# Second retention pair's queries and keys as one seven-product group, with the input sums formed in the first pair

## The chip, the cores and the metric

The kernel runs on one core of a Trainium2 chip. The metric is the device time of one execution in microseconds; the kernel before took 1776.57 us (median of 3 runs, 1776.14 to 1777.71). The engines of the core are named as in the profile: PE (matmul) and PEld (its weight loads), DVE (vector), ACT (activation), POOL (GpSimd) and SP, from whose queue the weights are loaded.

## What is computed

A trunk of two layers on 512 tokens of width 1024, in float32. A layer makes one combined projection `x @ w_in`, whose columns are split among two branches. The part that matters here is the retention branch with 4 heads of query and key width 128 and value width 256, which comes first in a layer:

```python
def _rotary(x, pos):
    half = x.shape[-1] // 2
    ...
    x1, x2 = x[..., :half], x[..., half:]
    return jnp.concatenate([x1 * cos - x2 * sin, x1 * sin + x2 * cos], axis=-1)
...
rq = _rotary(r_q.astype(f32).reshape(B, S, RET_HEADS, RET_QK_DIM), pos)
rk = _rotary(r_k.astype(f32).reshape(B, S, RET_HEADS, RET_QK_DIM), pos) * (RET_QK_DIM ** -0.5)
rv = r_v.astype(f32).reshape(B, S, RET_HEADS, RET_V_DIM)
o_ret = _head_norm(_retention(rq, rk, rv), ret_norm_g[l]) * jax.nn.silu(r_g.astype(f32))
```

The second branch (mLSTM) has queries and keys from a causal convolution, values, and an input and a forget gate per head (`m_i`, `m_f`, from the same projection). Both branches are gated, projected, added, normalised, and followed by a SwiGLU block and a second normalisation.

## The kernel before, in words

**Three matmuls for one.** Each float32 operand is split into a high part (a copy in the matmul's reduced format: `xh`, `whi`) and a low part (the difference: `xl`, `wlo`). A product is the sum of three matmuls: high by high, high by low, low by high (lines 266 to 268, 324, 357 to 359). ACT makes the high parts (line 201), DVE the low parts (`lo_of`, line 133).

**Weight units.** All weights lie in DRAM as units of 128 x 1024 (512 KB), in the order of use (`layer_plan`). A feature unit (`feat`, line 272) gives 128 output features for all 512 tokens: 24 matmuls of 512 columns into one PSUM bank, with a slot (below) after every sixth. A token unit (`tok_units`, line 361) is used by four blocks of 128 tokens: 6 matmuls and one slot for each block. `take` and `used` (lines 231 and 237) keep a ring of 5 raw and 5 prepared weight tiles running, some 4 units ahead.

**Seven products instead of eight.** `quad` (line 304) computes four feature units as a 2 x 2 block product with seven products in place of eight (in the manner of Strassen and Winograd). It loads four blocks of weights in place of four units (`QUADS`, `QUAD_BLOCKS`), forms three weight sums on DVE (lines 187, 189, 191) and one on POOL (line 223), and prepares seven operands in place of four. A product has 24 matmuls of 256 columns and two slots. On the other side it needs four sums of the input, `xs` (`input_sums`, line 580). A callback `ev` combines the banks after each product. Inside a quad the instructions of ACT, DVE and POOL keep the order of the program (`manual_schedule(engines=ordered)`). Before the change the quad is used for the mLSTM's queries and keys, for the two merge gates and for the SwiGLU units.

**The input sums.** `input_sums` is a generator with four groups (m = 0 to 3). Each group first adds high and low parts on POOL (2 instructions of line 586, tile `xs`), yields, then forms four sums on DVE (4 instructions of line 592, tile `sf`), casts them on ACT (line 593, `xs0h` in layer 0, `xs1h` in layer 1), takes the low half on DVE (line 133, `xs0l`, `xs1l`) and yields again.

**Order of the work.** PE and SP run in program order. On ACT, DVE and POOL a planner at compile time orders the instructions by its own estimate of when each is ready, and prefers the ones that stand earlier in the program. Smaller work is put between the matmuls by slots: `slot()` (line 246) takes the next step of a queue `side` and, at every `SLOW`-th slot, one step of a queue `slow`. `drain()` empties `side`. Only the input sums use `slow`.

**A layer's retention.** Heads go in pairs, p = 0 and 1. For a pair: four feature units (q, k of either head), each rotated out of its PSUM bank (`rot_evac`, lines 615 to 617 on DVE, 618 on POOL); for p = 0 the gate unit (`feat_if`) with a long chain of small operations on tile `rows` (`if_evac`, lines 632 to 662); four value token units (value stage), whose four PSUM banks are evacuated by ACT (`rvh`) and DVE (`rvl`); four gate token units (gate stage), into the same four banks of the pool `psm`, evacuated by ACT (line 732). Meanwhile `side` holds the first head's scores (`scores`, line 456), for p = 0 twelve empty steps and the transposes of the gate rows (`if_cols`, line 668), and in the gate stage the weighted sums of the first head, the scores of the second head and its weighted sums (`weighted`, line 495). The head norm of a pair (`head_norms`, with 16 transposes on line 547) runs in the slots of whatever comes next. The input sums are queued at the start of p = 1 and used first by the mLSTM's first quad.

Of the kernel before, what the change touches and what calls it, by code (L numbers as in the profile page):

```python
# [13 lines left out]
ALU = mybir.AluOpType  # L14

P = 128
S = 512
# [36 lines left out]
def layer_plan():  # L54
# [34 lines left out]
    for j in range(2, FT, 2):  # L89
        for c in (0, DFF):  # L90
# [5 lines left out]


NUNIT = len(layer_plan())
QUADS = [layer_plan().index(("F", w, c + j * P)) for w, c, js in (("in", O_MQK, (0, 2)), ("in", O_GA, (0, 4)),
                                                                  ("in", O_GB, (0, 4)), ("gu", 0, range(2, FT, 2))) for j in js]  # L100
UNIT_IF = layer_plan().index(("F", "if", 0))

# [2 lines left out]
def decoder_trunk(ctx: ExitStack, tc: tile.TileContext, wall, xT_in, x_in, pvec, lnp, rtab, out):  # L105
    nc = tc.nc
# [17 lines left out]
    def scratch(shape, name):  # L124
        return reg.tile(shape, F32, tag="sc", name=name, bufs=4)
# [12 lines left out]
    for l in range(L):  # L138
        i = 0
# [100 lines left out]


    side, slow = deque(), deque()
    SLOW = 5
    turn = {"n": 0}

    def slot():
# [333 lines left out]
    def input_sums(xh, xl, sh, sl):  # L580

        t1, t2 = slice(0, S // 2), slice(S // 2, S)
        for m in range(4):
            t = scratch([P, 2, S], "xs")
            for i in range(2):
                nc.gpsimd.tensor_tensor(out=t[:, i], in0=xh[:, m + 4 * i].bitcast(F32), in1=xl[:, m + 4 * i].bitcast(F32), op=ALU.add)
            yield
            f = scratch([P, 4, S // 2], "sf")
            a11, a12, a21, a22 = t[:, 0, t1], t[:, 1, t1], t[:, 0, t2], t[:, 1, t2]
            for i, a, b, op in ((0, a21, a22, ALU.subtract), (1, f[:, 0], a11, ALU.subtract),  # L590
                                (2, a11, a21, ALU.subtract), (3, f[:, 1], a12, ALU.add)):
                nc.vector.tensor_tensor(out=f[:, i], in0=a, in1=b, op=op)
            nc.scalar.copy(sh[:, :, m], f)
            lo_of(sl[:, :, m], f, sh[:, :, m])
            yield

    def rest(n):
        for _ in range(n):
            yield

    for l in range(L):
# [7 lines left out]
        xs = sum_views(oth, f"xs{l}")  # L609
        od = [dr.tile([P, KT, S], F32, tag=f"od{i}", name="od") for i in range(2)]  # L610

        def rot_evac(dst):
            def ev(pm):
                t = scratch([P, S], "rt")
                nc.vector.tensor_tensor(out=dst, in0=pm, in1=tab[:, 0], op=ALU.mult)
                nc.vector.tensor_tensor(out=t[0:64], in0=pm[64:128], in1=tab[0:64, 1], op=ALU.mult)
                nc.vector.tensor_tensor(out=t[64:128], in0=pm[0:64], in1=tab[64:128, 1], op=ALU.mult)
                nc.gpsimd.tensor_tensor(out=dst, in0=dst, in1=t, op=ALU.add)
            return ev

        def split_evac(vh, vl, hh, b, src):
            nc.scalar.copy(vh, src)
# [48 lines left out]
            yield  # L671

        for p in range(2):
            if p == 1:
                slow.append(input_sums(xh, xl, *xs))
            qk = reg.tile([P, 4, S], F32, tag="qk", name="rqk")
            rots = [rot_evac(qk[:, i]) for i in range(4)]
            if p == 0 and l > 0:
                feat_split(xh, xl, rots, between)
            elif p == 0:  # L680
                first_units(rots)
            else:
                for ev in rots:
                    feat(xh, xl, ev)
            if p == 0:
                feat_if(xh, xl, if_evac)
            boxes = [[None], [None]]

            def ret_weights(h):
# [62 lines left out]
                                               op0=ALU.mult, op1=ALU.add)  # L752
            nc.scalar.activation(x, t, AF.Silu)

        def conv_ev(qk):
            t = {}
            part = lambda i, h: qk[:, 2 * i : 2 * i + 2, h * HC : (h + 1) * HC]
            two = lambda bank: bank.rearrange("p (j t) -> p j t", j=2)

            def ev(name, banks):  # L760
                if name == "p1":
                    t["u"] = scratch([P, 2, 2, HC], "mu")
                    nc.scalar.copy(t["u"][:, 0], two(banks["a"]))
                elif name == "p5":
                    nc.scalar.copy(t["u"][:, 1], two(banks["c"]))
                elif name == "p7":
                    nc.vector.tensor_tensor(out=part(1, 1), in0=t["u"][:, 1], in1=two(banks["d"]), op=ALU.subtract)
                elif name == "p6":
                    u, v = t["u"][:, 0], t["u"][:, 1]
                    nc.vector.tensor_tensor(out=u, in0=two(banks["b"]), in1=u, op=ALU.add)  # L770
                    nc.gpsimd.tensor_tensor(out=v, in0=v, in1=u, op=ALU.subtract)
                    nc.gpsimd.tensor_tensor(out=part(1, 1), in0=part(1, 1), in1=u, op=ALU.subtract)
                elif name == "p2":
                    nc.scalar.copy(part(0, 0), two(banks["a"]))
                    nc.vector.tensor_tensor(out=part(1, 0), in0=two(banks["e"]), in1=t["u"][:, 1], op=ALU.add)
                elif name == "p4":
                    nc.vector.tensor_tensor(out=part(0, 1), in0=two(banks["d"]), in1=t["u"][:, 0], op=ALU.add)
            return ev

        for p in range(2):  # L780
            qk = reg.tile([P, 4, S], F32, tag="qk", name="mqk")
            with tc.manual_schedule(engines=ordered):
                quad(xh, xl, *xs, conv_ev(qk))
            for i in range(4):
                conv(qk[:, i], (i % 2) * 4 + 2 * p + i // 2)
            side.append(rest(7))
# [444 lines left out]
```

## Time and profile before

| | |
|---|---|
| median of 3 runs | 1776.57 us (1776.14 to 1777.71) |
| the profiled execution | 1777.92 us, span 1776.2 us |
| PE busy | 1759.9 us of the span |
| DVE busy | 1312.9 us |
| ACT busy | 793.6 us |
| POOL busy | 433.3 us |
| mean granted clock of PE | 0.998 |

The profile is of one execution. Its span runs from the first to the last instruction, and the execution's own time lies a little above it. In timelines a row has the start, the duration (both in us), the engine, the line of the kernel, the operation and its tiles, and, in brackets, how long the engine stood idle in front of it and what released it. Matmuls overlap, so the distance between the starts of two rows tells their rate, not the duration. In the views of groups the durations are in ns.

### The profile page before, as it was taken

Reading aid. Unit: us, or ns where it says so; the run is one execution under the profiler, and the core shown is the slowest. Engines: PE = TensorE matmul, PEld = TensorE weight load, DVE = VectorE, ACT = ScalarE, POOL = GpSimd, SP = SyncE. Lnnn points to the kernel's source line nnn. Section 1 sums busy time; section 2 is a strip of 40 time slices with the busy share of each in tenths; the row PEclk is TensorE's granted clock in tenths of the full one; section 3 lists DMA queues with packets and bytes.
Section 4 is the critical chain, followed back from the end, with each engine's and each line's share of the span. In section 5 each row is a group of like instructions: output and inputs, shape, how many; then the busy total and the mean of one; then the engine's idle time right before and its main releaser. Section 6 shows DMA issues by size and latency. Waiting matters only on the chain.

```text
span 1776.2 us, 27128 instructions
## 1 busy us (share of the span) xinstructions
PE 1759.9 (99%) x10904; PEld 1586.3 (89%) x10904; DVE 1312.9 (74%) x1726; ACT 793.6 (45%) x1148; POOL 433.3 (24%) x321
## 2 busy tenths in 40 slices
PE   9999999999999999999999999999999999999997
PEld 7888898998889999988898898989988899999886
DVE  6676878795559999963476968787845699998534
ACT  4445555663226444451244455556533254445310
POOL 2141110231001555520121311113300115555200
PEclk9999999999999999999999999999999999999999
DMA  7232422346333323363242323313553223333521
GB/s 250 86 105 72 143 72 96 106 137 239 96 111 110 105 96 108 107 213 95 83 166 89 110 88 106 119 60 108 200 180 119 95 95 108 111 116 114 186 69 48
DMA packets 74878, 209.48 MB, mean 118 GB/s; under 512 B 6616, under 2 KB 8536, under 8 KB 73728
## 3 DMA queue, kind: packets, MB, share of 16 engines
q1 hardware_dynamic: 64912, 168.32, 29.6%
q0 software_dynamic: 9840, 39.43, 6.3%
q8 instruction: 86, 1.41, 0.3%
q14 instruction: 40, 0.33, 0.1%
HBM read 190.93 MB, written 16.79 MB: 117 GB/s over the span
## 4 chain that ended last, share of the span: by engine, by line
PE 97%; DVE 1%; ACT 0%; issue 0%; DMA 0%; SPq 0%; DVEq 0%
PE pm L324 31%; PE pm L357 9%; PE pm L359 9%; PE pm L358 9%; PE pm L266 6%; PE pm L268 6%; PE pm L267 6%; PE pa L324 5%; PE pa L358 3%; PE pa L357 3%; PE pa L359 3%; PE pa L491 1%; PE pa L492 1%; PE pa L493 1%; PE pa L547 1%; PE pa L465 1%
## 5 line engine op out<-in xcount | busy, mean ns | idle before, releaser
L133 DVE TENSOR_TENSOR wlo<-wraw,whi 128x1024 fp32r<-128x1024 f32 (+2 forms) x416 | 599.6, 1453 | 203.1 <-ACT whi L201 200.5
L201 ACT CAST whi<-wraw 128x1024 fp32r<-128x1024 f32 x403 | 421.1, 1049 | 476.2 <-PE pm L267 116.0
L447 POOL TENSOR_TENSOR rs<-ve,nhalf 128x4 f32<-128x4 f32 (+1 forms) x32 | 33.0, 1033 | 480.2 <-DVE ve L446 480.2
L223 POOL TENSOR_TENSOR wraw<-wraw 128x1024 f32<-128x1024 f32 x32 | 77.0, 2405 | 150.9 <-issue 58.1
L357 PE MATMUL pm<-whi,x0h 128*128 128x512 f32 x256 | 102.5, 400 | 1.8 <-DVE rvl L133 1.7
L357 PE MATMUL pm<-whi,x20h 128*128 128x512 f32 x256 | 102.5, 400 | 0.6 <-DVE rvl L133 0.6
L359 PE MATMUL pm<-wlo,x0h 128*128 128x512 f32 x256 | 100.3, 392 | 0.0
L359 PE MATMUL pm<-wlo,x20h 128*128 128x512 f32 x256 | 100.3, 392 | 0.0
L358 PE MATMUL pm<-whi,x20l 128*128 128x512 f32 x256 | 100.1, 391 | 0.0
L358 PE MATMUL pm<-whi,x0l 128*128 128x512 f32 x256 | 100.1, 391 | 0.0
L1082 POOL TENSOR_TENSOR qa<-qa 128x512 f32<-128x512 f32 x20 | 42.8, 2142 | 142.3 <-DVE qa L1081 90.4
L324 PE MATMUL pm<-x10h,whi 128*128 128x256 f32 x240 | 67.9, 283 | 0.0
L324 PE MATMUL pm<-x10l,whi 128*128 128x256 f32 x240 | 67.9, 283 | 0.0
L324 PE MATMUL pm<-s0h,whi 128*128 128x256 f32 x240 | 67.9, 283 | 0.0
L324 PE MATMUL pm<-s0l,whi 128*128 128x256 f32 x240 | 67.9, 283 | 0.0
L324 PE MATMUL pm<-s0h,wlo 128*128 128x256 f32 x240 | 67.9, 283 | 0.0
L324 PE MATMUL pm<-x11h,whi 128*128 128x256 f32 x240 | 67.9, 283 | 0.0
L324 PE MATMUL pm<-x11l,whi 128*128 128x256 f32 x240 | 67.9, 283 | 0.0
L324 PE MATMUL pm<-x11h,wlo 128*128 128x256 f32 x240 | 67.9, 283 | 0.0
L324 PE MATMUL pm<-s1h,whi 128*128 128x256 f32 x240 | 67.9, 283 | 0.0
L324 PE MATMUL pm<-s1l,whi 128*128 128x256 f32 x240 | 67.9, 283 | 0.0
L324 PE MATMUL pm<-s1h,wlo 128*128 128x256 f32 x240 | 67.9, 283 | 0.0
(519 smaller groups left out, 5672.5 us busy)
## 6 DMA issues: line engine op xcount, KB each, us to landing
wraw<-wall SPq DMA_DIRECT2D x307, 512.0 KB, 3.8
od<-ot POOLq DMA_DIRECT2D x16, 512.0 KB, 3.6
of<-od POOLq DMA_DIRECT2D x16, 512.0 KB, 4.8
gb<-lnp POOLq DMA_DIRECT2D x4, 1024.0 KB, 6.3
x1d<-xr POOLq DMA_DIRECT2D x8, 512.0 KB, 3.0
xr<-x1d POOLq DMA_DIRECT2D x8, 512.0 KB, 4.6
negm<-md POOLq DMA_DIRECT2D x2, 1026.0 KB, 6.3
xr<-xtok POOLq DMA_DIRECT2D x4, 512.0 KB, 7.4
```

Source lines behind the costliest of these rows:

```text
L133: nc.vector.tensor_tensor(out=out_lo, in0=full, in1=hi.bitcast(F32), op=ALU.subtract)
L201: nc.scalar.copy(hi, sum_t[i])
L223: nc.gpsimd.tensor_tensor(out=raw_t[u + 2], in0=raw_t[u], in1=raw_t[u + 3], op=ALU.add)
L266: nc.tensor.matmul(pm[:, c0:c1], lhsT=hi[:, k], rhs=xh[:, k, c0:c1], start=(k == 0), stop=False)
L267: nc.tensor.matmul(pm[:, c0:c1], lhsT=hi[:, k], rhs=xl[:, k, c0:c1], start=False, stop=False)
L268: nc.tensor.matmul(pm[:, c0:c1], lhsT=lo[:, k], rhs=xh[:, k, c0:c1], start=False, stop=(k == KT - 1))
L324: nc.tensor.matmul(pm, lhsT=x[:, j, k], rhs=y[:, k], start=go and n == 0, stop=j == 1 and k == 3 and n == 2, skip_group_check=not first)
L357: nc.tensor.matmul(pm, lhsT=sh(k)[:, a], rhs=hi[:, j], start=first, stop=False)
L358: nc.tensor.matmul(pm, lhsT=sl(k)[:, a], rhs=hi[:, j], start=False, stop=False)
L359: nc.tensor.matmul(pm, lhsT=sh(k)[:, a], rhs=lo[:, j], start=False, stop=last)
L447: nc.gpsimd.tensor_tensor(out=rs[:, :n], in0=ve[:, :n], in1=nhalf[:, :n], op=ALU.pow)
L1082: nc.gpsimd.tensor_tensor(out=v, in0=v, in1=u, op=ALU.subtract)
```

## The change

The four feature units of the second retention pair (p = 1) become one `quad`. The callback that was `conv_ev` is now called `blocks_ev`, stands earlier in the layer and is used for both; it leaves the plain queries and keys in `qk`. After the quad the four are rotated in place, from SBUF, by the new `rotate`, which `rot_evac` of the first pair uses too, with the products of the swapped halves first. Seven empty steps (`rest(7)`) are put into `side` before the scores, as the mLSTM has them. The quad's units are added to `QUADS`, so that its weights are loaded in blocks. Since the quad needs the input sums, these are queued in p = 0, right after `feat_if`, and with a step at every third slot in place of every fifth; an assertion says that they are queued completely before the quad.

```diff
-QUADS = [layer_plan().index(("F", w, c + j * P)) for w, c, js in (("in", O_MQK, (0, 2)), ("in", O_GA, (0, 4)),
+QUADS = [layer_plan().index(("F", w, c + j * P)) for w, c, js in (("in", O_RQ, (2,)), ("in", O_MQK, (0, 2)), ("in", O_GA, (0, 4)),
...
-    SLOW = 5
+    SLOW = 3
...
+        def blocks_ev(qk):
...
+        def rotate(dst, x):
+            t = scratch([P, S], "rt")
+            nc.vector.tensor_tensor(out=t[0:64], in0=x[64:128], in1=tab[0:64, 1], op=ALU.mult)
+            nc.vector.tensor_tensor(out=t[64:128], in0=x[0:64], in1=tab[64:128, 1], op=ALU.mult)
+            nc.vector.tensor_tensor(out=dst, in0=x, in1=tab[:, 0], op=ALU.mult)
+            nc.gpsimd.tensor_tensor(out=dst, in0=dst, in1=t, op=ALU.add)
+
         def rot_evac(dst):
-            def ev(pm):
-                t = scratch([P, S], "rt")
-                nc.vector.tensor_tensor(out=dst, in0=pm, in1=tab[:, 0], op=ALU.mult)
...
+            return lambda pm: rotate(dst, pm)
...
         for p in range(2):
-            if p == 1:
-                slow.append(input_sums(xh, xl, *xs))
...
             else:
-                for ev in rots:
-                    feat(xh, xl, ev)
+                assert not slow
+                with tc.manual_schedule(engines=ordered):
+                    quad(xh, xl, *xs, blocks_ev(qk))
+                for i in range(4):
+                    rotate(qk[:, i], qk[:, i])
+                side.append(rest(7))
             if p == 0:
                 feat_if(xh, xl, if_evac)
+                slow.append(input_sums(xh, xl, *xs))
...
-        def conv_ev(qk):
...
-                quad(xh, xl, *xs, conv_ev(qk))
+                quad(xh, xl, *xs, blocks_ev(qk))
```

The callback, unchanged but for its name and place:

```python
def blocks_ev(qk):
    t = {}
    part = lambda i, h: qk[:, 2 * i : 2 * i + 2, h * HC : (h + 1) * HC]
    two = lambda bank: bank.rearrange("p (j t) -> p j t", j=2)
    def ev(name, banks):
        if name == "p1":
            t["u"] = scratch([P, 2, 2, HC], "mu")
            nc.scalar.copy(t["u"][:, 0], two(banks["a"]))
        elif name == "p5":
            nc.scalar.copy(t["u"][:, 1], two(banks["c"]))
        elif name == "p7":
            nc.vector.tensor_tensor(out=part(1, 1), in0=t["u"][:, 1], in1=two(banks["d"]), op=ALU.subtract)
        elif name == "p6":
            u, v = t["u"][:, 0], t["u"][:, 1]
            nc.vector.tensor_tensor(out=u, in0=two(banks["b"]), in1=u, op=ALU.add)
            nc.gpsimd.tensor_tensor(out=v, in0=v, in1=u, op=ALU.subtract)
            nc.gpsimd.tensor_tensor(out=part(1, 1), in0=part(1, 1), in1=u, op=ALU.subtract)
        elif name == "p2":
            nc.scalar.copy(part(0, 0), two(banks["a"]))
            nc.vector.tensor_tensor(out=part(1, 0), in0=two(banks["e"]), in1=t["u"][:, 1], op=ALU.add)
        elif name == "p4":
            nc.vector.tensor_tensor(out=part(0, 1), in0=two(banks["d"]), in1=t["u"][:, 0], op=ALU.add)
    return ev
```

More of the change, by code (lines that the diff above doesn't have):

```diff
@@ L610, in decoder_trunk, with ev @@
         od = [dr.tile([P, KT, S], F32, tag=f"od{i}", name="od") for i in range(2)]
-        def rot_evac(dst):
-            def ev(pm):
-                t = scratch([P, S], "rt")
[L615 to L619, printed above, removed]
+        def blocks_ev(qk):
+            t = {}
+            part = lambda i, h: qk[:, 2 * i : 2 * i + 2, h * HC : (h + 1) * HC]
+            two = lambda bank: bank.rearrange("p (j t) -> p j t", j=2)
+            def ev(name, banks):
+                if name == "p1":
+                    t["u"] = scratch([P, 2, 2, HC], "mu")
+                    nc.scalar.copy(t["u"][:, 0], two(banks["a"]))
+                elif name == "p5":
+                    nc.scalar.copy(t["u"][:, 1], two(banks["c"]))
+                elif name == "p7":
+                    nc.vector.tensor_tensor(out=part(1, 1), in0=t["u"][:, 1], in1=two(banks["d"]), op=ALU.subtract)
+                elif name == "p6":
+                    u, v = t["u"][:, 0], t["u"][:, 1]
+                    nc.vector.tensor_tensor(out=u, in0=two(banks["b"]), in1=u, op=ALU.add)
+                    nc.gpsimd.tensor_tensor(out=v, in0=v, in1=u, op=ALU.subtract)
+                    nc.gpsimd.tensor_tensor(out=part(1, 1), in0=part(1, 1), in1=u, op=ALU.subtract)
+                elif name == "p2":
+                    nc.scalar.copy(part(0, 0), two(banks["a"]))
+                    nc.vector.tensor_tensor(out=part(1, 0), in0=two(banks["e"]), in1=t["u"][:, 1], op=ALU.add)
+                elif name == "p4":
+                    nc.vector.tensor_tensor(out=part(0, 1), in0=two(banks["d"]), in1=t["u"][:, 0], op=ALU.add)
+            return ev
@@ L753, in conv @@
             nc.scalar.activation(x, t, AF.Silu)
-        def conv_ev(qk):
[L756 to L778, printed above, removed]
         for p in range(2):
```

## The prediction

> **What bounds the kernel now.** I read the page's first part first, then the matrix engine's waits, then timelines of the places that the diff touches, then a table of busy time by stretches.
>
> ```profile
> span 1776.2 us, 27128 instructions
> PE 1759.9 (99%) x10904; PEld 1586.3 (89%) x10904; DVE 1312.9 (74%) x1726; ACT 793.6 (45%) x1148; POOL 433.3 (24%) x321
> ```
>
> PE is busy for all but 16.3 us of the span. So the kernel can get faster by little except by less matrix work, and it gets slower by every microsecond in which another engine lets PE wait. Where PE waits for another engine today, the waits view says in its first row:
>
> ```profile
> PE pm L357 <- DVE rvl L133: 2.3, 2, 1.7
> ```
>
> Two waits, one per layer, both of the same kind: the first matmul of the gate units of the first retention pair waits for DVE, which still has to write the low half of the values (rvl) before the PSUM bank is free. The PE timeline at that place, first layer, then second layer:
>
> ```profile
> 59.49 0.39 PE L359 MATMUL pm<-wlo,x0h 128*128 128x512 f32 x1
> 60.09 0.44 PE L668 MATMUL pa<-ident,rows 36*128 36x36 f32 x4 [0.21 <-DVE rows L659]
> 62.27 0.50 PE L357 MATMUL pm<-whi,x0h 128*128 128x512 f32 x1 [1.74 <-DVE rvl L133]
> ```
> ```profile
> 941.60 0.50 PE L357 MATMUL pm<-whi,x20h 128*128 128x512 f32 x1 [0.58 <-DVE rvl L133]
> ```
>
> And DVE in front of it (first layer):
>
> ```profile
> 49.74 0.68 DVE L644 TENSOR_TENSOR rows<-rows 4x512 f32<-4x512 f32 x1 [2.47 <-ACT rows L643]
> ...
> 61.55 1.87 DVE L133 TENSOR_TENSOR rvl<-pm,rvh 128x512 fp32r<-128x512 f32 x3
> ```
>
> DVE runs the long chain of the input and forget gates there (rows), and around it the low halves of the weights. Busy time by stretch (columns: PE, PEld, DVE, ACT, POOL, clock, DMA): value stage of pair 0 in layer 0, gate stage of pair 0, the first seven-product group of the mLSTM, value stage of pair 0 in layer 1.
>
> ```profile
> 36.00:61.50 25.50, 24.24 (x111) 19.56 (x109) 22.21 (x36) 14.46 (x20) 5.34 (x4) 1.00 0.40 127
> 66.00:94.00 28.00, 28.00 (x153) 24.15 (x152) 15.75 (x38) 13.05 (x25) 3.97 (x4) 1.00 0.23 74
> 171.40:193.30 21.90, 21.90 (x186) 21.90 (x185) 15.19 (x19) 14.16 (x22) 4.13 (x4) 1.00 0.55 163
> 916.00:941.00 25.00, 25.00 (x116) 20.47 (x114) 20.77 (x35) 14.63 (x20) 3.45 (x4) 1.00 0.32 105
> ```
>
> In the value stage of pair 0 DVE has 3.29 us free of 25.5 (layer 0) and 4.23 us of 25.0 (layer 1), and PE is already waiting for it at the end: this is the one stage in which DVE, not PE, ends last. In the gate stage it has 12.25 us free. The clock is 1.00 throughout and is no part of the argument.
>
> **Part 1: four feature units become a seven-product group.** The four units of pair 1 issue 4 x 24 = 96 matmuls of 512 columns, the group 7 x 24 = 168 of 256; 16 transposes of the head norm of the pair before (L547) lie inside either. The group of the first mLSTM pair stands between the same neighbours (gate units before, value units after), so its duration is the price:
>
> ```profile
> 93.30 0.39 PE L266 MATMUL pm<-x0h,whi 128*128 128x512 f32 x1
> ...
> 116.97 0.39 PE L357 MATMUL pm<-whi,x0h 128*128 128x512 f32 x1
> ...
> 171.24 0.28 PE L324 MATMUL pm<-x0h,whi 128*128 128x256 f32 x1
> ...
> 193.05 0.48 PE L357 MATMUL pm<-whi,x0h 128*128 128x512 f32 x1
> ```
>
> Four units: 116.97 - 93.30 = 23.67 us. A group: 193.05 - 171.24 = 21.81 us. Gain 1.86 us per layer, 3.72 us in two layers, which run the same instructions. That is all PE can win: an eighth fewer columns, but 72 more matmuls.
>
> The Trainium skill ("TensorE: Matmul & The Clock Gate", Back-to-back issue gap) prices a matmul in a stream at its columns over 2.4 GHz and 2.5 ns more; by that the gain would be 96 x 215.8 - 168 x 109.2 ns = 2.4 us per layer. The rows above give 1.86, and they decide.
>
> What the group adds beside PE per layer: three more casts on ACT, three more low halves and three weight sums on DVE, one on POOL, copies and sums of the blocks; the loads are the same 512 KB each, cut into blocks, in the same ring. The third row of the table is the cover: all this ran beside the first mLSTM group with PE busy 21.90 of 21.90 us. If it ran short there, PE would wait inside the group; nothing of that is seen in any of the four mLSTM groups, whose conv behind them is heavier than a rotation. Two of the weight sums fall into the gate stage of pair 0:
>
> ```profile
> L187 DVE TENSOR_TENSOR wraw<-wraw 128x1024 f32<-128x1024 f32 x32 | 39.0, 1218 | 0.0
> ```
>
> 2 x 1.2 = 2.4 us of the 12.25 free. Cost 0 on the path.
>
> **Part 2: rotation from SBUF, after the group.** Rotations ran after each unit, from PSUM; now four run in a row behind the group, in place. Nothing shows a rotation from SBUF. Its multiplies as they are now:
>
> ```profile
> L616 DVE TENSOR_TENSOR rt<-pm,rtab x16: 692/693/694, 26.5 to 997.2; 64x512 f32<-64x512 f32 x16
> L617 DVE TENSOR_TENSOR rt<-pm,rtab x16: 683/684/685, 27.2 to 997.9; 64x512 f32<-64x512 f32 x16
> L618 POOL TENSOR_TENSOR rqk<-rqk,rt x16: 1287/2314/2336, 28.0 to 998.7; 128x512 f32<-128x512 f32 x16
> ```
>
> With the first multiply at the same 0.69 us, one is 2.07 us on DVE. The first query and key are ready about 0.7 + 4.1 + 2.3 = 7.1 us behind the group. The change puts seven empty steps (rest) and the unfinished head norm in front of the scores, just as the mLSTM does, where the first score matmul comes at
>
> ```profile
> 205.40 0.59 PE L465 MATMUL pa<-mqk 128*128 128x256 f32 x2
> ```
>
> 12.35 us behind the group's end (193.05). 5 us are left over; cost 0. The steps in front of the gate units are then 15 + 7 + 3 = 25 of 30 slots, so the weighted sums start where they start now, and the table of decays comes free for the mLSTM's row maxima (negm) as before.
>
> **Part 3: the input sums move from pair 1 to pair 0.** Per layer 8 additions on POOL, 16 on DVE, 4 casts on ACT, 4 low halves on DVE; no DMA. In POOL's queue they now stand among the two small stores of the gate rows and the head norm's powers, which nobody waits for within the stage. On DVE one of the four groups costs, by medians:
>
> ```profile
> L592 DVE TENSOR_TENSOR sf<-xs x16: 410/420/1512, 101.1 to 1013.4; 128x256 f32<-128x256 f32 x16
> L592 DVE TENSOR_TENSOR sf<-sf,xs x16: 409/412/416, 102.8 to 1013.8; 128x256 f32<-128x256 f32 x16
> L593 ACT CAST xs0h<-sf x4: 1053/1054/1055, 104.8 to 135.7; 128x1024 fp32r<-128x1024 f32 x4
> L133 DVE TENSOR_TENSOR xs0l<-sf,xs0h x4: 1210/1222/1406, 105.8 to 137.1; 128x1024 fp32r<-128x1024 f32 x4
> ```
>
> 2 x 0.420 + 2 x 0.412 + 1.222 = 2.89 us. With SLOW = 3 there is a step at every third slot behind feat_if, and every second step is a DVE step: in layer 0 the first group's stands at the 6th of the 16 slots of the value units, the second's at the 12th (in layer 1 up to two slots earlier), both in program order ahead of the value evacuations of the last unit (slots 13 to 16). The third and fourth fall among the gate units. DVE's order is made by a planner that prefers what stands earlier in the program; that sums really go in front of an evacuation is seen in pair 1 now, where the sums' low half splits the rotation of a unit:
>
> ```profile
> 104.65 0.68 DVE L615 TENSOR_TENSOR rqk<-pm,rtab 128x512 f32<-128x512 f32 x1
> 105.85 1.41 DVE L133 TENSOR_TENSOR xs0l<-sf,xs0h 128x1024 fp32r<-128x1024 f32 x1 [0.52 <-ACT xs0h L593]
> 107.28 0.69 DVE L616 TENSOR_TENSOR rt<-pm,rtab 64x512 f32<-64x512 f32 x1
> ```
>
> There PE had other work; in pair 0 it has none: behind the last value matmul come only the 4 transposes of the gate rows (which wait for the rows chain) and gate units (which wait for rvl). So two groups, 5.77 us, come in front of rvl. The POOL additions also slow DVE where both read SBUF:
>
> ```profile
> 124.75 2.93 POOL L586 TENSOR_TENSOR xs<-x0h,x0l 128x512 f32<-128x512 f32 x2 [3.88 <-DVE xs0l L133]
> ```
> ```profile
> 126.45 2.31 DVE L133 TENSOR_TENSOR wlo<-wraw,whi 128x1024 fp32r<-128x1024 f32 x1
> ```
>
> A low half took 2.31 us beside them against 1.22, so 1.09 us per pair of additions, 2.18 us for two. The Trainium skill ("SBUF — State Buffer", SBUF: two separate sides) says that these two engines share one pair of ports, held for a whole instruction. By that rule such a delay is to be expected, and the two rows agree.
>
> Bounds per layer: at best no collision and all free DVE time filled, 5.77 - 3.29 = 2.48 us and 5.77 - 4.23 = 1.54 us, 4.0 us together; at worst 5.77 + 2.18 = 7.95 us each and nothing filled, 15.9 us. I take the collisions, since DVE is nearly always busy there, and let the one real gap (2.47 us, while ACT works) be filled: 7.95 - 2.47 = 5.48 us. That gap is three quarters of layer 0's free time; three quarters of 4.23 is 3.17, so layer 1 gives 7.95 - 3.17 = 4.78 us. Together 10.26 us, nearest to the row with the gap. ACT (14.46 of 25.5 busy) takes the two casts without loss. What pair 1 gets back on DVE is worth nothing, since PE doesn't wait there.
>
> **Sum.** 10.26 - 3.72 = +6.5 us. The profiled execution took 1777.92 us, 1.72 around its span of 1776.2, and lies 1.35 us over the median of the three runs (1776.57). On its own time the sum gives 1784.5 us, on the median 1783.1. About 0.2% (3.5 us) is what a measurement of this kernel can tell from no change.
>
> **Rivals.** *The sums find room elsewhere*, and the change is not slower: the planner puts the DVE steps behind rvl or into earlier gaps. For it: the gate stage has 12.25 us free, and sums have run ahead of their place. Against it: they stand earlier in the program than rvl. It gives 1776.57 - 3.72 = 1772.9 us if all is hidden, and up to 1776.9 with the best bound (4.0 us). It decides if the wait that is added at the first gate unit stays under 1.86 us per layer; up to 3.6 us (1.86 and half of 3.5) the change still can't be told from none. Chance 0.22.
>
> *A second wait in the gate stage*: third and fourth group delay the second head's scores. There is little slack where PE begins the weighted sums:
>
> ```profile
> 81.98 0.35 DVE L480 SCALAR_TENSOR_TENSOR pp<-pa,pv,pp 128x128 fp32r<-128x128 f32 x1 [0.43 <-ACT pp L479]
> ...
> 82.73 0.29 PE L491 MATMUL pa<-rvh,pp 128*128 128x256 f32 x1
> ```
>
> 82.73 - 82.33 = 0.40 us. One group in front of it costs 2.89 - 0.40 = 2.5 us, 5.0 in two layers: 1788.1 us. Against it are the free 12.25 us, into which 5.77 + 2.18 + 2.4 us go. It decides once more than 0.40 us of sums lies between the scores and line 480. Chance 0.12.
>
> *The rotation comes late*: POOL's additions and DVE's multiplies in SBUF hinder each other. It decides at 12.35 us; were all twelve multiplies delayed by 1.09 us, the first two would be ready at 7.1 + 6 x 1.09 = 13.6 us, 1.3 us late per layer, on top of the forecast 1785.7 us. Chance 0.04.
>
> **Chances and range.** The forecast has 0.62, of which 0.12 ends under +3.5 us (its best bound is +0.3). The first rival splits into 0.09 faster by over 0.2% (only if all is hidden) and 0.13 within. So faster 0.09, within 0.2% 0.25, slower 0.66. The range 1774.0 to 1789.0 us leaves out the wholly hidden case below (0.10) and the upper ends of forecast and second rival (0.09); the forecast's own range is 1776.9 to 1788.8.
>
> **What would show it.** Right: no L266 rows in pair 1 and 21.8 us for its group; PE's wait for rvl before the first gate unit at about 7 us (layer 0) and 5 us (layer 1), with sf and xs0l rows on DVE before rvl; PE busy time down by about 4 us, span up. Wrong: sf rows behind rvl with unchanged waits (first rival), PE waits at L491 (second) or at L465 of pair 1 (third), or any wait inside the new group, which would overturn part 1.

## The result, and the profile after

The changed kernel takes 1789.81 us (median of six runs, 1787.58 to 1792.62), the kernel before beside it 1777.14 us (six runs, 1776.14 to 1780.74): a ratio of 1.0063, 95% interval 1.0053 to 1.0073. It is slower, by 11 us by the ratio. The profiled execution took 1789.91 us. First the head of its page, then the first rows of the view of PE's waits:

```profile
span 1788.2 us, 27473 instructions
PE 1761.9 (99%) x11048; PEld 1594.7 (89%) x11048; DVE 1330.0 (74%) x1746; ACT 800.2 (45%) x1160; POOL 449.2 (25%) x327
```
```profile
PE pa L694 <- DVE rows L685: 9.2, 2, 5.4
PE pm L357 <- DVE rvl L133: 2.5, 4, 1.1
...
PE pa L492 <- DVE rvl L133: 1.0, 1, 1.0
```

The span is 12.0 us longer, although PE was to need 3.7 us less. PE's busy time has not fallen but risen by 2.0 us: something makes PE's own work slower. And the transposes of the gate rows, which before waited 0.2 us for DVE in the first layer and not at all in the second (L668 then, L694 now), wait 9.2 us in the two. PE's timeline at these places, first layer and second layer:

```profile
65.47 0.64 PE L694 MATMUL pa<-ident,rows 36*128 36x36 f32 x4 [5.43 <-DVE rows L685]
67.18 0.80 PE L357 MATMUL pm<-whi,x0h 128*128 128x512 f32 x1 [1.08 <-DVE rvl L133]
...
950.29 0.64 PE L694 MATMUL pa<-ident,rows 36*128 36x36 f32 x4 [3.75 <-DVE rows L685]
952.00 0.79 PE L357 MATMUL pm<-whi,x20h 128*128 128x512 f32 x1 [1.08 <-DVE rvl L133]
956.77 0.39 PE L492 MATMUL pa<-rvl,pp 128*128 128x256 f32 x1 [0.99 <-DVE rvl L133]
```

The same place of the first layer by stretches of two microseconds, with the same columns as before (behind the busy times of the five engines stands the granted clock):

```profile
62.00:64.00 2.00, 0.00 (x0) 0.00 (x0) 2.00 (x3) 0.00 (x0) 2.00 (x2) 1.00 0.80 250
...
66.00:68.00 2.00, 0.92 (x3) 0.72 (x3) 2.00 (x5) 1.44 (x3) 1.84 (x3) 0.50 0.03 8
...
70.00:72.00 2.00, 2.00 (x9) 1.85 (x8) 2.00 (x3) 0.37 (x1) 0.21 (x1) 0.50 0.00 0
72.00:74.00 2.00, 2.00 (x11) 1.70 (x10) 2.00 (x6) 0.50 (x2) 0.00 (x0) 0.95 0.66 207
```

PE stands still, DVE and POOL are busy without a gap. When PE goes on, its clock is 0.50 until about 72, and its matmuls of 512 columns start 0.43 us apart instead of 0.23. What DVE did up to the end of the wait (some of its rows), and POOL beside it:

```profile
49.90 1.07 DVE L670 TENSOR_TENSOR rows<-rows 4x512 f32<-4x512 f32 x1 [0.63 <-ACT rows L669]
...
58.58 1.19 DVE L133 TENSOR_TENSOR xs0l<-sf,xs0h 128x1024 fp32r<-128x1024 f32 x1
...
60.91 1.74 DVE L680 TENSOR_TENSOR_SCAN rows<-rows,mp 4x256 f32<-4x256 f32 x1
62.57 0.39 DVE L592 TENSOR_TENSOR sf<-xs 128x256 f32<-128x256 f32 x1
62.89 1.74 DVE L684 SCALAR_TENSOR_TENSOR rows<-rows 4x512 f32<-4x512 f32 x1
64.56 0.41 DVE L592 TENSOR_TENSOR sf<-sf,xs 128x256 f32<-128x256 f32 x1
64.99 0.42 DVE L685 COPY rows<-rows 4x512 f32<-4x512 f32 x1
```
```profile
60.13 0.53 POOL L688 DMA_DIRECT2D md<-mp  x1 [9.71 <-DVE mp L683]
60.67 3.41 POOL L586 TENSOR_TENSOR xs<-x0h,x0l 128x512 f32<-128x512 f32 x2
```

Sums stand between the steps of the rows chain (xs0l at 58.58 belongs to the first group, the two sf rows to the second), and two steps of the chain take 1.74 us while POOL forms the third group's additions. That these meet the chain's last steps is no accident: in POOL's order they follow the store `md<-mp`, for which POOL stood idle 9.71 us, and this store waits for a step of the same chain (L683). The seven-product group itself:

```profile
100.48 0.28 PE L324 MATMUL pm<-x0h,whi 128*128 128x256 f32 x1
...
122.29 0.48 PE L357 MATMUL pm<-whi,x0h 128*128 128x512 f32 x1
```

122.29 - 100.48 = 21.81 us, in both layers, and no wait inside.

**Where the 12.0 us are.** From the starts of the first matmul of each stage (before to after):

| stage | layer 0 | layer 1 |
|---|---|---|
| pair 0, value and gate stage | 57.28 to 64.05: +6.77 | 55.51 to 62.93: +7.42 |
| pair 1, queries and keys | 23.67 to 21.81: -1.86 | 23.67 to 21.81: -1.86 |
| pair 1, value and gate stage | 54.27 to 54.84: +0.57 | 54.25 to 54.81: +0.56 |

With 0.41 us at the program's start this is 12.01 us (that start differs from profile to profile: the value stage begins at 36.43 us here, and between 34.48 and 37.77 in the experiments). Nearly all of the loss is in the first pair. Of its 14.19 us the added waits are (5.43 + 1.08) - (0.21 + 1.74) = 4.56 us in layer 0 and (3.75 + 1.08 + 0.99) - 0.58 = 5.24 us in layer 1, 9.80 together. That leaves 4.39 us, 2.2 per layer, and PE's rows at the low clock account for about as much: the starts of the first 18 matmuls of the gate stage of layer 0 span 5.63 us (67.18 to 72.81) where they spanned 3.36 (62.27 to 65.63), those of the first 10 of layer 1 span 3.36 where they spanned 1.86, and the transposes take 0.64 us in place of 0.44 in either layer, 4.2 us together.

### The profile page after: what moved, and what is told of

It reads as the page before. It is cut to its first block, busy times and chain, and to the rows that moved or that the text cites. A ratio compares the mean times of both kernels' runs of the same rounds, so it can differ in the third digit from the quotient of the medians.

```text
span 1788.2 us, 27473 instructions
## 1 busy us (share of the span) xinstructions
PE 1761.9 (99%) x11048; PEld 1594.7 (89%) x11048; DVE 1330.0 (74%) x1746; ACT 800.2 (45%) x1160; POOL 449.2 (25%) x327
## 4 chain that ended last, share of the span: by engine, by line
PE 93%; DVE 4%; issue 1%; ACT 1%; DMA 1%; SPq 0%; DVEq 0%; ACTq 0%
PE pm L324 33%; PE pm L357 9%; PE pm L359 9%; PE pm L358 9%; PE pa L324 5%; PE pm L267 4%; PE pm L268 4%; PE pm L266 4%; PE pa L358 3%; PE pa L357 3%; PE pa L359 3%; PE pa L492 1%; PE pa L491 1%; PE pa L493 1%; DVE wlo L133 1%
## 5 line engine op out<-in xcount | busy, mean ns | idle before, releaser
L201 ACT CAST whi<-wraw 128x1024 fp32r<-128x1024 f32 x409 | 427.2, 1049 | 478.5 <-PE pm L267 112.6
L223 POOL TENSOR_TENSOR wraw<-wraw 128x1024 f32<-128x1024 f32 x34 | 81.8, 2405 | 171.7 <-issue 58.2
L324 PE MATMUL pm<-x10h,wlo 128*128 128x256 f32 x240 | 67.9, 283 | 0.0
```

What stands on the lines that cost most here:

```text
L201: nc.scalar.copy(hi, sum_t[i])
L223: nc.gpsimd.tensor_tensor(out=raw_t[u + 2], in0=raw_t[u], in1=raw_t[u + 3], op=ALU.add)
L324: nc.tensor.matmul(pm, lhsT=x[:, j, k], rhs=y[:, k], start=go and n == 0, stop=j == 1 and k == 3 and n == 2, skip_group_check=not first)
```

## The experiments

The theory after reading the trace: the group gains what was forecast, and the input sums in the first pair cost some 15 us, by waits for DVE and by the clock behind them. Open were which part of the sums makes the wait (DVE's own work or POOL's additions beside it), whether the place matters, and what the clock does. The rivals stand in the expectations. Stage times below are those of pair 0's value and gate stage, layer 0 and layer 1 (before 57.28 and 55.51 us, after 64.05 and 62.93).

**The sums alone: `e1_sums_only`.** The kernel before, with the sums queued in the first pair:

```diff
-    SLOW = 5
+    SLOW = 3
...
-            if p == 1:
-                slow.append(input_sums(xh, xl, *xs))
...
                 feat_if(xh, xl, if_evac)
+                slow.append(input_sums(xh, xl, *xs))
```

> Part 3 alone: the input sums move to pair 0 with a step at every third slot; the second pair keeps its four feature units. My theory (two groups of sums on DVE in front of the gate rows and of rvl stop PE by 9.8 us in two layers, and PE's clock is halved behind each of these waits, 4.4 us more) expects about +14 us against the kernel before, 1791 us (1788 to 1794), with PE's waits for rows or rvl of about 5 us in either layer. The rival (the new group and its preparation in the gate stage are what costs, the sums are nearly free) expects 1777 us, within 3 us of before.

Measured: 1794.11 us (1791.56 to 1795.62) against 1778.43, ratio 1.0087 (1.0073 to 1.0101); stages 64.60 and 64.41 us; the time lies just over the expected 1788 to 1794. PE's waits:

```profile
PE pa L668 <- DVE rows L659: 8.7, 2, 5.4
PE pm L357 <- DVE rvl L133: 5.2, 2, 4.1
```

The waits are there without any group or new rotation: moving the sums alone costs about 15.5 us (0.0087 x 1778).

**No sums: `f1_no_sums`.** The group and the rotation alone:

```diff
-        xs = sum_views(oth, f"xs{l}")
+        xs = tuple(t.rearrange("p (s m) (c t) -> p s (m c) t", s=4, c=2) for t in (xh, xl))
...
-                slow.append(input_sums(xh, xl, *xs))
```

> The changed kernel without any input sums, in the first pair or anywhere: the sums' operations are left out, and the groups of the second retention pair and of both mLSTM pairs read views of the plain input in their place, so its matmuls, evictions and rotations are those of the change and its numbers are not. Theory (the loss is the wait that the moved sums cause in the first pair, and the clock's drop behind it): 1771 us (1768 to 1775), with the second pair's group still at 21.8 us per layer, no wait above 0.5 us at the transposes of the gate rows, and no stretch of halved clock. Rival (the group with its rotation in place costs by itself): at or above the 1777 us of the kernel before.

Measured: 1774.99 us (1773.47 to 1776.86) against 1778.38, ratio 0.9978 (0.9970 to 0.9987), a gain of 3.9 us by the ratio, at the upper end of the expected 1768 to 1775 us; stages 57.05 and 55.40 us, about as before; the groups took 21.81 and 21.79 us. From DVE's timeline of layer 0, the rows chain from the step that waits for ACT to the last step before PE's transposes:

```profile
47.96 0.68 DVE L670 TENSOR_TENSOR rows<-rows 4x512 f32<-4x512 f32 x1 [2.48 <-ACT rows L669]
...
56.35 0.74 DVE L680 TENSOR_TENSOR_SCAN rows<-rows,mp 4x256 f32<-4x256 f32 x1
57.12 0.68 DVE L684 SCALAR_TENSOR_TENSOR rows<-rows 4x512 f32<-4x512 f32 x1
57.84 0.42 DVE L685 COPY rows<-rows 4x512 f32<-4x512 f32 x1
```

57.84 - 47.96 = 9.88 us, and the transposes still wait 0.2 us for it (1.7 us more for rvl). So the chain of this layer had no slack: whatever lengthens it lengthens PE's wait one for one. In the changed kernel the same stretch is 64.99 - 49.90 = 15.09 us, 5.21 longer, and the wait there is 5.43 - 0.21 = 5.22 us longer.

**One half of the sums at a time: `f3_no_pool` and `f2_pool_only`.** In the first DVE forms the sums from the high part of the input directly and POOL has nothing to add (the low part is left out of the sums). In the second POOL's additions stay and nothing is made of them, and the groups read views of the plain input.

```diff
 def input_sums(xh, xl, sh, sl):                      # f3_no_pool
...
-            t = scratch([P, 2, S], "xs")
-            for i in range(2):
-                nc.gpsimd.tensor_tensor(out=t[:, i], in0=xh[:, m + 4 * i].bitcast(F32), ...
             yield
             f = scratch([P, 4, S // 2], "sf")
-            a11, a12, a21, a22 = t[:, 0, t1], t[:, 1, t1], t[:, 0, t2], t[:, 1, t2]
+            a11, a12, a21, a22 = (xh[:, m + 4 * i, a].bitcast(F32) for a in (t1, t2) for i in range(2))
```
```diff
 def input_sums(xh, xl, sh, sl):                      # f2_pool_only
...
                 nc.gpsimd.tensor_tensor(out=t[:, i], in0=xh[:, m + 4 * i].bitcast(F32), ...
             yield
-            f = scratch([P, 4, S // 2], "sf")
...
-            nc.scalar.copy(sh[:, :, m], f)
-            lo_of(sl[:, :, m], f, sh[:, :, m])
             yield
```

> The changed kernel with VectorE's and ScalarE's part of the sums in its place, reading the hi part of the input directly, and without the GpSimd additions hi + lo. Theory (VectorE's own work, put between the chain's operations, makes the wait): the wait at the gate rows' transposes stays at 3 us or more, total 1785 us (1781 to 1789). Rival (contention with GpSimd's additions makes it): VectorE's subtraction rows at 0.42 us, scans at 0.74 us, a wait under 1 us, total 1775 us or less.

Measured: 1785.38 us (1783.25 to 1787.76), ratio 1.0038 (1.0026 to 1.0050), 10.4 us over the kernel without sums; stages 61.32 and 61.49 us. The expected wait of 3 us or more came in layer 0 (3.0) and not in layer 1 (1.6). Two rows of DVE's timeline, then PE's waits:

```profile
49.69 0.68 DVE L667 TENSOR_TENSOR rows<-rows 4x512 f32<-4x512 f32 x1 [2.47 <-ACT rows L666]
...
62.33 0.42 DVE L682 COPY rows<-rows 4x512 f32<-4x512 f32 x1
```
```profile
PE pa L691 <- DVE rows L682: 4.6, 2, 3.0
PE pm L357 <- DVE rvl L133: 4.3, 4, 2.9
```

The chain is 12.64 us long: DVE's own sums make 12.64 - 9.88 = 2.76 us of the 5.21 in layer 0. The other 2.45 us are POOL's doing: from this kernel to the changed one, the scan goes from 0.74 to 1.74 us, L684 from 0.68 to 1.74 and L670 from 0.68 to 1.07, 2.45 together.

> The changed kernel with the eight GpSimd additions of each layer's sums in their place in the first pair, and without VectorE's and ScalarE's part of the sums; the groups read views of the plain input. Theory (VectorE's own 2.9 us per group, put between the chain's operations, make most of the wait): the gate rows' transposes wait under 2 us, total 1773 us (1770 to 1778). Rival (the GpSimd additions slow the chain's VectorE operations, and that alone makes the wait): scans at 1.7 us, a wait of 3 us or more and a total of 1781 us or more.

Measured: 1785.89 us (1784.72 to 1786.91), ratio 1.0039 (1.0027 to 1.0052); stages 63.42 and 59.22 us. DVE, POOL and PE's waits:

```profile
51.27 1.54 DVE L133 TENSOR_TENSOR pp<-pf,pp 128x384 fp32r<-128x384 f32 x1
52.73 0.34 DVE L480 SCALAR_TENSOR_TENSOR pp<-pa,pv,pp 128x128 fp32r<-128x128 f32 x1
```
```profile
41.48 12.48 POOL L586 TENSOR_TENSOR xs<-x0h,x0l 128x512 f32<-128x512 f32 x8
```
```profile
PE pa L687 <- DVE rows L678: 5.6, 2, 4.5
PE pm L357 <- DVE rvl L133: 3.9, 4, 1.7
```

My expectation that POOL alone would cost little fell: it costs 10.9 us over the kernel without sums. With nothing of DVE between them, all eight additions run in one piece beside the front of the chain. The low half of a score takes 1.54 us there (0.56 in the kernel without sums), while L480, which reads a PSUM bank, takes its usual 0.34 us in the midst of it. Each half alone costs 10 to 11 us, both together 14.8 (1789.81 - 1774.99), so the halves don't add up. Additions that run in one piece hit other steps: here the chain from L663 to L678 takes its 9.88 us again and only begins late (54.28). And the low clock lasts as long behind the shorter waits of the kernel without POOL's additions (6.83 us in either layer) as in the changed kernel. How much each of the two reasons accounts for was not separated.

**Later steps: `e5_slow4`.** Would it help if by the program only the first group's sums stood in front of all four value evacuations, and the third group's additions behind the value units?

```diff
-    SLOW = 3
+    SLOW = 4
...
-                assert not slow
+                while slow:
+                    if next(slow[0], "end") == "end":
+                        slow.popleft()
```

> The changed kernel with a step of the sums at every fourth slot (rest of them forced ahead of the group). In layer 0 the first group's DVE step is then at slot 6 of the value units and the second's at slot 14, behind the evacuations of the first two blocks. Theory (each group in front of rvl costs 2.9 us and a collision): some 4 us less wait per layer, and waits short enough that the clock stays: 1778 us (1775 to 1783). Rival (the order of rows chain and POOL sets the wait, not the number of groups): above 1786 us.

Measured: 1788.70 us (1786.54 to 1789.28), ratio 1.0056 (1.0043 to 1.0069); the expected 1778 us did not come, and the first wait is unchanged:

```profile
PE pa L694 <- DVE rows L685: 9.3, 2, 5.5
```

The number of slots doesn't decide. Up to the transposes the planner put the sums where they stand in the changed kernel: the third group's additions run at 60.67 us in both, although by the program they now belong to the gate stage.

**Queued one stage later: `e7_gate2`, and with manual order: `g1_gate_pinned`.**

```diff
-    SLOW = 3
+    SLOW = 2
...
                 feat_if(xh, xl, if_evac)
-                slow.append(input_sums(xh, xl, *xs))
...
             tok_units([main_bank() ...], ..., v_evac)
+            if p == 0:
+                slow.append(input_sums(xh, xl, *xs))
```

(Steps that are left when the group begins are taken in front of it, as in `e5_slow4`.) The second:

```diff
         if slow and turn["n"] % SLOW == 0:           # g1_gate_pinned, on top of that
-            if next(slow[0], "end") == "end":
+            with tc.manual_schedule(engines=ordered):
+                end = next(slow[0], "end") == "end"
+            if end:
                 slow.popleft()
```

> The changed kernel with the sums queued one stage later, behind the value units of the first pair and in front of its gate units, at every second slot. Theory (the sums hurt only because VectorE's chain of gate rows and the value evictions stand behind them in the value stage): no wait at the gate rows' transposes, rows at 0.74 us for the scans, total 1773 us (1769 to 1780). Rival (the sums cost VectorE's and GpSimd's time wherever they are put): a wait of 2 us or more in the gate stage or at the group, total 1783 us or more.

> The changed kernel with the sums queued behind the first pair's value units, at every second slot, and each of their steps held at its place in the written order on ScalarE, VectorE and GpSimd, so that nothing of them is brought forward into the value stage. Theory (the sums cost what they delay in the value stage, where VectorE's chain of gate rows has no slack; the gate stage has VectorE free time of about 11.5 us for their 11.6 us): wait at the gate rows' transposes back to 0.2 us, clock 1.00 there, waits of up to 3 us per layer in the gate stage, total 1778 us (1774 to 1783). Rival (the sums cost their time on VectorE and GpSimd in any place of the first pair): total 1787 us or more.

Measured: 1791.78 us, ratio 1.0072 (1.0059 to 1.0084), stages 66.73 and 62.68 us; and 1791.77 us, ratio 1.0075 (1.0063 to 1.0088), stages 66.09 and 62.67 us. From DVE's timeline and PE's waits of the first of the two:

```profile
54.39 0.43 DVE L592 TENSOR_TENSOR sf<-xs 128x256 f32<-128x256 f32 x1
```
```profile
PE pa L493 <- DVE pp L480: 4.7, 2, 2.4
PE pa L694 <- DVE rows L685: 4.2, 2, 3.0
```

Neither kernel did what it was made for: the first sums run at 54 us, in the value stage, although they are queued behind it. In the second they run at 54.22 us and POOL's additions stand as in the first, so the manual order of single steps changed nothing. The later place did move the third and fourth group: their additions run at 83.40 and 87.14 us in place of 60.67 and 66.69, and the transposes wait 4.2 us in place of 9.2. But a new wait takes the place of this gain, 2.4 us per layer at L493 in the gate stage, for the second head's key weights.

**Held back by a dependence: `h1_gate_held`.** The place and the slots of `e7_gate2`, and POOL first writes a few columns of each scratch tile from the last value tile:

```diff
-    def input_sums(xh, xl, sh, sl):
+    def input_sums(xh, xl, sh, sl, late):            # late = vl[:, 3, 1, :4].bitcast(F32)
...
             t = scratch([P, 2, S], "xs")
+            for i in range(2):
+                nc.gpsimd.tensor_tensor(out=t[:, i, :4], in0=late, in1=late, op=ALU.add)
```

> The changed kernel with the sums queued behind the first pair's value units and held there by a dependence: GpSimd writes four columns of each sums' scratch tile from the pair's last value tile first (two small additions per group more), so no sum can start before the value stage is evicted. Theory (the sums cost what they delay in the value stage, where VectorE's chain of gate rows has no slack): wait at the gate rows' transposes back to 0.2 us, clock 1.00 there, the first pair's two stages at 57 to 60 us; waits of up to 2.4 us per layer where the second head's weights (pp) are read; total 1779 us (1775 to 1783). Rival (the sums cost their time on VectorE and GpSimd in any place of the first pair): total 1786 us or more.

Measured: 1790.08 us (1788.39 to 1790.60) against 1777.05, ratio 1.0068 (1.0054 to 1.0082); stages 63.68 and 62.54 us. PE's waits, and PE's timeline of layer 0:

```profile
PE pa L493 <- DVE pp L480: 6.4, 2, 3.2
PE pm L357 <- DVE rvl L133: 2.6, 4, 1.7
```
```profile
61.22 0.44 PE L696 MATMUL pa<-ident,rows 36*128 36x36 f32 x4 [0.23 <-DVE rows L687]
63.40 0.63 PE L357 MATMUL pm<-whi,x0h 128*128 128x512 f32 x1 [1.74 <-DVE rvl L133]
63.83 0.63 PE L358 MATMUL pm<-whi,x0l 128*128 128x512 f32 x1
...
89.52 0.39 PE L493 MATMUL pa<-rvh,pp 128*128 128x256 f32 x1 [3.19 <-DVE pp L480]
```

This time the hold worked, and the value stage's waits are those of the kernel without sums. Yet the time is the same: in the gate stage the second head's key weights come late, by 3.2 us in each layer, with the clock at 0.50 behind it (from 91 to 94 us in layer 0). My theory that only the value stage is the wrong place fell; the rival holds for all places tried in the first pair. And there is a surprise at 63.40: the wait of 0.23 and 1.74 us that the kernel before has too (0.21 and 1.74), with the clock at 1.00 behind it there, is followed here by matmuls 0.43 us apart, half the clock.

**Sums behind the group: `e2_quad_only` and `e2_again`.** Is the move needed? Here the real sums are queued in the second pair, behind the rotations; the pair's group reads views of the plain input.

```diff
-                    quad(xh, xl, *xs, blocks_ev(qk))
+                    quad(xh, xl, *xsub, blocks_ev(qk))   # xsub: views of xh, xl
                 for i in range(4):
                     rotate(qk[:, i], qk[:, i])
                 side.append(rest(7))
+                slow.append(input_sums(xh, xl, *xs))
...
                 feat_if(xh, xl, if_evac)
-                slow.append(input_sums(xh, xl, *xs))
```

> Parts 1 and 2 alone: the seven-product group and the rotation in place, but the group multiplies with views of the plain input in place of the input sums (wrong queries and keys for the second pair, the same work); the real sums are formed behind the group, in pair 1, a step at every third slot. My theory expects the gain of the group and nothing else: 1777 - 3.7 + up to 1 us, so 1774 us (1772 to 1777), with PE's waits for rvl as in the kernel before. The rival (the group costs) expects over 1785 us.

> The kernel of the run e2_quad_only once more, for a profile that can be read. If the sums behind the group make it 25 us slower than the kernel before: waits for rvl or for the scores of the second pair of 5 us or more in its value stage in each layer, with VectorE busy with rotations and sums, and stretches of halved clock behind them. If the rotation or the group does: a longer group than 21.8 us.

Measured: ratio 1.0136 (1.0120 to 1.0153), about 24 us slower; and 1803.10 us in the one execution of the second run. PE's waits and DVE's timeline of the second:

```profile
PE pm L357 <- DVE rvl L133: 23.6, 4, 10.7
```
```profile
118.67 0.68 DVE L639 TENSOR_TENSOR rt<-rqk,rtab 64x512 f32<-64x512 f32 x1
...
128.80 1.66 DVE L640 TENSOR_TENSOR rt<-rqk,rtab 64x512 f32<-64x512 f32 x1
```

The expected gain (1774 us) did not come. The rotations (twelve multiplies) and the sums now meet in the second pair's value stage, and POOL's additions stretch the multiplies from 0.69 to 1.66 us; rvl of that pair is 10.7 us late in each layer. The stage that received the rotations can't hold the sums as well.

**The clock: `e3_fill` and `g2_fill_all`.** Matmuls that nobody reads are put into the changed kernel's wait, to see whether it is PE's standing still that brings the clock down:

```diff
             r3 = rows[:, 3]
+            idle = aux_bank()
+            for _ in range(16):                      # g2_fill_all: 25 if l == 0 else 18
+                nc.tensor.matmul(idle, lhsT=xh[:, 0, :P], rhs=xh[:, 0], start=True, stop=True)
             pa = aux_bank()
             for b in range(NB):
                 nc.tensor.transpose(pa[:, b * 36 : (b + 1) * 36], ...)
+            for _ in range(6):                       # g2_fill_all only
+                nc.tensor.matmul(idle, lhsT=xh[:, 0, :P], rhs=xh[:, 0], start=True, stop=True)
```

> The changed kernel with 16 matmuls of 512 columns more per layer, whose result nobody reads, in front of the transposes of the gate rows, where PE waits (3.6 us of work in waits of 3.75 and 5.43 us). Theory that the long idle time itself lowers PE's clock behind it: the clock stays near 1.00, and the time falls by about 4.4 us against the changed kernel, to 1785.5 us (1784 to 1787.5). Rival (the slow matmuls behind the wait have another cause, such as DVE and POOL at the same memory): 1790 us as before, since the filler hides in the wait.

> The changed kernel with idle matmuls of 512 columns in front of the gate rows' transposes (25 in layer 0, 18 in layer 1, about as many as fill the wait) and six behind them in each layer, so that TensorE hardly stands still at the border of value and gate stage; the idle matmuls write a bank that nothing reads. If TensorE's standing still brings the clock to 0.50 there: no such stretch, total 1786.5 us (1784 to 1789), 3 to 5 us below the changed kernel. If something else brings it down: the stretch stays, total 1790 us or more.

Measured: 1792.87 us, ratio 1.0078 (1.0063 to 1.0092), with waits of 1.88 and 1.28 us left in layer 0, 0.15 and 1.28 us in layer 1, and the clock at 0.50 behind them in both, so that this kernel filled only a part of the wait and doesn't separate the two; and 1795.20 us, ratio 1.0095 (1.0079 to 1.0110). The second one by stretches, and its next wait:

```profile
58.00:66.00 8.00, 8.00 (x39) 6.39 (x38) 7.94 (x12) 0.91 (x2) 4.21 (x4) 1.00 0.40 131
66.00:72.00 6.00, 6.00 (x32) 5.10 (x31) 6.00 (x9) 2.97 (x4) 3.87 (x3) 1.00 0.01 3
...
76.00:77.00 1.00, 1.00 (x7) 1.00 (x6) 1.00 (x2) 0.17 (x1) 0.00 (x0) 0.50 0.00 0
```
```profile
75.44 0.58 PE L491 MATMUL pa<-rvh,pp 128*128 128x256 f32 x1 [2.98 <-DVE cols L700]
```

Filled to the end, the wait leaves the clock at 1.00 (no stretch under it from 58 to 72, nor in layer 1 from 946 to 986), with DVE and POOL busy as before. So it is PE's standing still that lowers it. The time didn't follow: DVE's order changed with the added matmuls (the copy of the gate columns, at 71.82 us in the changed kernel, now runs at 75.10 behind sums), PE waits 2.98 us for it, and the low clock comes there. That the 4.4 us would come back if the clock stayed up is therefore not shown, only that the clock falls with the wait.

No version tried beats the kernel before with the sums really made.

## Why the prediction was right, and where not

The sign and, in the main, the mechanism were right: the moved sums make PE wait for DVE in the first pair for longer than the group gains. The forecast of +6.5 us was too small by 5.5 on the span (12.0). The median, 1789.81 us, lies 0.8 us above the range's upper end; by the ratio to the kernel before, run beside it, the forecast's 1776.57 us become 1787.8, which is inside.

- **Part 1, the group: right.** Forecast -3.72 us, measured -3.72 in the rows of the stage. The 2.4 us per layer that it works out beside this from the Trainium skill ("TensorE: Matmul & The Clock Gate", Back-to-back issue gap) were too high: the section calls that formula one for an isolated matmul, which under-counts small ones in a stream of weight loads and matmuls. In the rows of this stream the starts lie 0.227 us apart for 512 columns and 0.120 for 256, both above the formula. With the rotation and without sums the kernel gained 3.9 us (interval 2.3 to 5.3, from 0.0013 and 0.0030 times 1778).
- **Part 2, rotation at cost 0: nearly right.** No wait for the scores came. The second pair's value and gate stage is longer by 0.57 and 0.56 us, also without any sums (54.84 and 54.85 us there). Two of the twelve multiplies take 1.66 and 1.67 us in place of 0.69 beside the rotation's own additions on POOL (126.46 and 129.60 us in layer 0), which the forecast's 2.07 us for each rotation left out. Of the 0.57 and 0.56 us a new wait for rvl is 0.18 in layer 0 and 0.20 in layer 1; the rest lies between matmuls at the stage's start and middle and was not traced further. 1.1 us in all.
- **Part 3, the waits: right in sum, by another way, and so close by luck.** Forecast 10.26 us, measured 9.80; by layers 5.48 and 4.78 forecast, 4.56 and 5.24 measured. Two groups do stand in front of rvl. But most of the wait falls at the transposes of the gate rows, not at rvl: the first group and half of the second stand between the steps of the rows chain, behind its wait for ACT, and the forecast had them between the chain and rvl. The collisions were expected from the additions of the first two groups; those run beside low halves in front of L670 and for the most part found room in the gap there (0.63 us of its 2.47 are left). What counted was the third group's additions, beside the chain's last steps. The forecast put the third group among the gate units, but by its own count of slots (POOL's step three slots ahead of DVE's) these additions stand at the 15th of the 16 slots of the value units.
- **The step that failed**: "The clock is 1.00 throughout and is no part of the argument." That was read from a kernel whose longest wait here is 1.74 us. With the longer wait the clock fell to 0.50, 2.2 us per layer, 4.39 us in all. It is most of the 5.5 us missing; 1.1 from part 2 and 0.4 at the program's start, less the 0.46 by which the waits were smaller, are the rest.
- **First rival (the sums hidden)**: not what happened; either half of the sums alone already costs 10 us.
- **Second rival (a wait in the gate stage)**: absent from the changed kernel, but its mechanism is real. When the sums were held out of the value stage, the wait came where it was put (the product that reads pp after line 480) with 3.2 us per layer for a forecast of 2.5.
- **Third rival (the rotation late)**: no wait for scores came. Its mechanism is real: two multiplies in layer 0 of the changed kernel are stretched, and more of them where the sums run behind the group (`e2_again`), where rvl and not the scores comes late.

## What to carry to other kernels

Before moving work on an engine that "has free time", look at the end of the stage that receives it: a chain that another engine already waits for, if only by 0.2 us, has no slack, and what lengthens it lengthens the wait by as much (5.21 and 5.22 us here). Price a wait with the clock behind it, not only with its length; and price an addition on POOL with what it does to the two-operand SBUF work of DVE beside it. Where a planner orders the engines, look at the rows for the place where moved work really runs: a later place in the program moved only half of the sums here, and only a data dependence held all of them.

## What the runs showed of the hardware

**The clock behind a short wait.** From the start of the last matmul of the value units of layer 0 to that of the first of the gate units, with four small transposes between, 2.78 us passed in the kernel before and 2.80 in the one without sums, and the clock stayed at 1.00; with the same 2.80 us in `h1_gate_held` and 2.78 in `e2_again` it was 0.50 for 3.41 us behind. Layer 1 of `e3_fill` needed even less, 2.25 us, for the same 3.41, while a wait of 2.39 us between matmuls in layer 1 of `g2_fill_all` left it at 1.00. The low stretches of the changed kernel and of `h1_gate_held` in layer 0, cut to a tenth of a microsecond (the clock's mean is 0.51 because the edges lie inside):

```profile
65.30:72.20 6.90, 5.65 (x19) 4.75 (x20) 6.87 (x12) 3.39 (x6) 4.05 (x3) 0.51 0.01 2
```
```profile
63.60:67.10 3.50, 3.50 (x12) 2.91 (x12) 2.88 (x5) 0.22 (x1) 0.47 (x3) 0.51 0.47 150
```

All low stretches read in the retention stages last 3.41, 6.83 or 10.24 us: one, two or three times the same length (6.83 in both layers of the changed kernel, 10.24 in both of `e1_sums_only`). So the length of the wait does not set what the fall of the clock costs. The Trainium skill ("TensorE: Matmul & The Clock Gate", What's actually happening) says that a free-running window of about 3.4 us decides, so that it matters where in the window the pause falls. The rows agree with that: the low clock comes in multiples of 3.41 us, and the same pause falls into it in two kernels and not in two others; where a window began, no row shows. They don't agree with a whole idle window as the condition, which the same section gives, since 2.8 us of pause were enough.

**POOL's additions and DVE.** Beside them a scan over only 4 partitions took 1.74 us in place of 0.74, and the low half of a score over 128 partitions 1.54 in place of 0.56: a microsecond more either way, so a small instruction is no protection. An operation with one operand in PSUM took its 0.34 us as ever. The Trainium skill ("SBUF — State Buffer", SBUF: two separate sides) lets the two block each other, for a whole instruction, where DVE reads two operands from SBUF or runs in one of its two-port modes. The rows agree on two operands; the two-port modes were not looked at.
